# One decoder block on one core: a latent's spread in another PSUM group, two weight splits placed later, and the order of some additions and last sums

## The chip, the cores and the metric

The kernel runs on one core of one Trainium2 chip. The metric is the device time of one execution in microseconds (us). The kernel before took a median of 786.34 us in three runs (785.65 to 786.46).

## The reference, cut to what matters

One block of depth 1 on 512 tokens with a model width of 1024, everything in fp32:

```
n      = rmsnorm(x);  proj = n @ w_in            # gq gk gv gr, gates, cq, ckv, kr, z_ma, z_mb
y_gla  = rmsnorm(gla_forward + gla_backward) * silu(gr)          # 4 heads, dk 128, dv 256, chunked
q      = rmsnorm(cq) @ w_uq;  k, v = rmsnorm(ckv) @ w_ukv        # 8 heads, with rotary parts
y_mla  = softmax(q k^T) v
h      = x + (sigmoid(z_ma) * y_gla + sigmoid(z_mb) * y_mla) @ w_out
h      = h + square(relu(rmsnorm(h) @ w_ff1)) @ w_ff2            # 1024 -> 4096 -> 1024
out    = rmsnorm(h) * g_final
```

## The kernel before, in words

**Arithmetic.** fp32 operands are split into a high part (rounded by ScalarE, L96 or L100) and a low part (the rest, by VectorE, L97 or L101). A product is three matmuls: high by high, high by low, low by high (`mm3`, L91 to L93). So every weight tile passes through three steps: a load on SyncE's queue (`weights`, L222), a high half on ScalarE, a low half on VectorE. Staging buffers for raw weights (`wf`) are three; the halves (`wh`, `wl`) have four buffers each.

**Who orders the work.** The program is traced in the order of the code. A scheduler then orders each engine's instructions by priority and by when buffers come free, and adds the semaphore waits. The code overrides it in places: `issued_after` (L103) makes one instruction of an engine stand behind another, `in_program_order` (L113) holds a whole stretch to the traced order, and `tensor_engine_goes_on` (L126) puts TensorE's first instruction of one stretch behind its last one of another. Each engine and each queue runs its own list in order: an instruction that waits holds everything behind it on that engine.

**PSUM.** There are two groups of four banks, `mm` and `at` (`ps`, L80). Projections use `mm`. Scores, gates, sums of squares and the spread of a norm use `at`. A new tile of a group takes the bank whose last user is done.

**First part, per GLA head h = 0..3** (loop at L782). The head's gates come from `gate_parts`; `gla_qk` makes decayed q and k. Then follow `mla_g2` (a projection of z_mb, named zb, multiplied by R on VectorE, L532, and put through tanh on ScalarE, L534, named tb) and `gla_scores` (L476). `gla_scores` makes bd (four 128-column products), copies it to bds on ScalarE (L483), and then makes for each of four key tiles a score tile sc: three matmuls (L491 to L493), a compare-copy of the diagonal on VectorE (L497), and a split (L96, L97). In heads 0, 1 and 3 TensorE is held to zb first and the scores behind it; head 2 does it the other way round. After the scores come the next head's gates (gatef, gateb, L395), in heads 0 to 2.

**The latents** (`latent`, L584). In head 3 the key/value latent ckv and the query latent cq are projected, and the row norm is found by sums of squares, a power on GpSimd (L265) and a diagonal (cqdg, L273). `spread` (L279) multiplies the diagonal by ones so that every partition holds all norms (tile cqrs, a bank of `at`). VectorE multiplies cq by it (cqc, L602), the result is split (cqhl), and the rotary product ro and the query projections read it. The spread is held behind head 3's scores on TensorE. Also in head 3, VectorE makes the rotary keys (krsin, kswap, kr, L665 to L668).

**Output product, norm and transposes** (`rows_product`, L855). The merged rows times w_out, in two column halves, four row tiles i of 128 tokens. In the second half the last four k blocks are kept back, so that the row tiles complete one after another. On completion VectorE adds the tile to the residual h (L905), ScalarE squares, GpSimd takes the power (L182) and VectorE normalises into ms (L922); then TensorE transposes it (mb, L197). Two row tiles share the banks; `evacuate` writes the transposed activations mT, eight times, high on ScalarE (L100), low on VectorE (L101). TensorE goes straight into the first two MLP weight tiles f00 and f01 on the first half of the tokens, then the transposes of rows 2 and 3, then the second half. Tiles f02, f03 and so on follow with all tokens.

**MLP** (four quarters of the 4096 hidden features). Eight tiles f make the hidden activations (`hidden`, relu at L1000, squares behind it). The second product is done in seven block products on 2 x 2 blocks (`ORDER`, L1032), with weight tiles w that are combined and split by `prep`. Their sums gather in PSUM tiles gx, gz, gw and are added to h after each product (`add_rows`, L905). In the last quarter the split for product 2 is prepared after product 7; product 4 goes on in the same bank (gx) whose content product 7's addition reads.

**End** (`last_rows`, L1066, in program order). Products 4 and 2 are done by rows. For each row tile: addition, square of the left half, last sum and power (`row_rstd`, L178, on VectorE and GpSimd), then `out_store` (L1059): left half times norm and gain on VectorE (L1061), right half times norm on ScalarE (L1062), and two stores (L1063, L1064).

Of the kernel before, what the change touches and what calls it, by code (L numbers as in the profile page):

```python
# [15 lines left out]
ALU = mybir.AluOpType  # L16
AX = mybir.AxisListType

P = 128
S = 512  # L20
# [39 lines left out]
def tile_block(ctx: ExitStack, tc: tile.TileContext, t, out: bass.AP):  # L60
# [19 lines left out]
    def ps(tag, name):  # L80
        serial[0] += 1
        return pp.tile([P, S], F32, tag=tag, bufs=4, name=f"{name}_{serial[0]}")
# [39 lines left out]
            prev[ins.engine] = ins.name  # L122

    PE_ONLY = (mybir.EngineType.PE,)

    def tensor_engine_goes_on(start, mid):  # L126

        ins = nc.cur_bb.bb.instructions
        pe = [[i for i in part if i.engine in PE_ONLY] for part in (ins[start:mid], ins[mid:])]
        issued_after(pe[1][0], pe[0][-1].name)  # L130


    ident = one([P, P], F32, "ident")
# [142 lines left out]
            )  # L276
        return diag

    def spread(diag, name):  # L279
        rs = ps("at", f"{name}rs")  # L280
        for x in range(2):
            nc.tensor.matmul(
                rs, ones_r, diag[:, x].rearrange("p a b -> p (a b)"), start=x == 0, stop=x == 1
            )
        return rs
# [298 lines left out]
    def latent(col, n, gcol, name):  # L584
        cs, sqs = [], []
        for j in range(n):
            acc = proj_T(col + j * P, f"{name}{j}")
            c = u2(f"{name}c{j}")
            nc.scalar.activation(c, acc, AF.Copy, scale=gvec[:, gcol + j : gcol + j + 1])
            s = u2(f"{name}s{j}")  # L590
            nc.scalar.activation(s, acc, AF.Square)
            if sqs:
                nc.vector.tensor_tensor(s, s, sqs[-1], op=ALU.add)
            cs.append(c)
            sqs.append(s)
        yield
        diag = feature_rstd(sqs[-1], n * P, name, True)
        yield
        rs = spread(diag, name)
        res = []  # L600
        for j in range(n):
            nc.vector.tensor_tensor(cs[j], cs[j], rs, op=ALU.mult)  # L602
# [179 lines left out]
    for h in range(GH):  # L782
        last = h == GH - 1
        if h:
            g1 = gla_g1(h, (0,))
            waiting = gla_rstd(*waiting)
            g1 += gla_g1(h, (1,))
            y1 += gla_norm(*waiting)
        if h == GH - 2:
            cos, sin = rotary_tables()  # L790
        near, nxt, far = gla_qk(h, parts)
        if last:
            ckv_steps, cq_steps = latent(C_CKV, 2, V_KV, "ckv"), latent(C_CQ, 3, V_Q, "cq")
# [7 lines left out]
        begun = traced()  # L801
        if h == 2:
            sc = gla_scores(near, nxt, far)
            g2.append(mla_g2(2 * h))
        else:
            g2.append(mla_g2(2 * h))
            gated_at = traced()
            sc = gla_scores(near, nxt, far)
            tensor_engine_goes_on(begun, gated_at)
        if last:  # L810
            scored_at = traced()
            cq = next(cq_steps)
            tensor_engine_goes_on(gated_at, scored_at)
# [41 lines left out]
    def rows_product(lhs, w, nk, name, first_done, done, flip):  # L855
        for c in range(2):
            accs = [ps(("mm", "at")[c], f"{name}{c}{i}") for i in range(NT)]

            def piece(i, k2, wh, wl):
                tok = slice(i * P, (i + 1) * P)  # L860
                for kk in range(2):
                    k = 2 * k2 + kk
                    mm3(accs[i], lhs[k][:, 0, tok], lhs[k][:, 1, tok], wh[:, kk, :], wl[:, kk, :],
                        k == 0, k == nk - 1)

            staggered = 2 if c == 1 else 0
# [24 lines left out]

            whole, first, rest = slice(0, 4), slice(0, 2), slice(2, 4)
            for i in range(2):
                part(i, whole)
# [17 lines left out]
    def first_half_square(i):  # L912
        hparts[i] = sm(f"hp{i}", 4)
        ms_rows[i] = u4(f"ms{i}", F32, (P, D))
        square_half(hrow[i], 0, hparts[i], ms_rows[i])

    def normed(i):
        m = ms_rows[i]
        square_half(hrow[i], 1, hparts[i], m)
        rs = row_rstd(hparts[i])  # L920
        for c in range(2):
            nc.vector.tensor_scalar(  # L922
                m[:, c * S : (c + 1) * S], hrow[i][:, c * S : (c + 1) * S], rs, None, op0=ALU.mult
            )

    def flipped(i):
        fm.rows(i, ms_rows[i])
        if i % 2 == 1:
            fm.evacuate(i // 2)

    begun = rows_product(merged, t["w_out"][0], KD, "wo", first_half_square, normed, flipped)


# [59 lines left out]
    def hidden(qd, j):  # L993

        if qd == 0 and j < 2:
            acc = early[j][2]
        else:
# [54 lines left out]
    def out_square(i, cols, final=True):  # L1052
# [3 lines left out]
            return row_rstd(p)  # L1056
        nc.vector.scalar_tensor_tensor(p[:, 2:3], p[:, 1:2], 1.0 / D, p[:, 2:3], op0=ALU.mult, op1=ALU.add)

    def out_store(i):  # L1059
        o, rs = ms_rows[i], hparts[i][:, 3:4]  # L1060
        nc.vector.scalar_tensor_tensor(o[:, 0:S], hrow[i][:, 0:S], rs, gfin[:, 0:S], op0=ALU.mult, op1=ALU.mult)  # L1061
        nc.scalar.activation(o[:, S:D], o[:, S:D], AF.Copy, scale=rs)  # L1062
        nc.sync.dma_start(out[0, i * P : (i + 1) * P, 0:S], o[:, 0:S])  # L1063
        (nc.scalar if i == 1 else nc.sync).dma_start(out[0, i * P : (i + 1) * P, S:D], o[:, S:D])  # L1064

    def last_rows(left, right4, right2, x_accs):  # L1066
# [6 lines left out]
        e_accs = [ps("mm", f"ge{rb}") for rb in range(2)]  # L1073
        parts = e_accs[1], ps("at", "gend")
        block_product(2, left, right2, e_accs, True, 0)
        out_store(2)
        add_rows(0, 0, e_accs[0])
        out_square(0, slice(0, S))
        out_store(3)
        cols = [slice(x * HT, (x + 1) * HT) for x in range(2)]  # L1080
        for x in range(2):
# [20 lines left out]
    for qd in range(NQ):  # L1102
# [14 lines left out]
        for n, m in enumerate(ORDER):  # L1117
# [50 lines left out]
```

## Time and profile before

| what | value |
|---|---|
| median of three runs | 786.34 us |
| the profiled execution | 786.52 us |
| its span, first to last instruction | 784.8 us |
| TensorE's mean granted clock | 0.997 |
| TensorE busy | 773.0 us |
| VectorE busy | 546.6 us |
| ScalarE busy | 409.9 us |
| GpSimd busy | 103.7 us |

The span is what the trace covers; the time of the execution has 1.7 us more. Engines are named PE (TensorE), PEld (its weight loads), DVE (VectorE), ACT (ScalarE), POOL (GpSimd) and SP (SyncE); a q behind the name is the engine's sequencer, which also issues transfers. A row of a timeline has the start in us from the span's begin, the duration, the engine, the line of the kernel, the operation, out<-in by the program's names, the shape, how many such instructions the row holds, and in brackets the idle time of the engine before it with what ended it. Matmul ends are modelled, so two rows may overlap; the distance from one start to the next is what a matmul costs when nothing waits.

### The profile page before, as it was taken

Reading aid. Unit: us, or ns where it says so; the run is one execution under the profiler, and the core shown is the slowest. Engines: PE = TensorE matmul, PEld = TensorE weight load, DVE = VectorE, ACT = ScalarE, POOL = GpSimd, SP = SyncE. Lnnn points to the kernel's source line nnn. Section 1 sums busy time; section 2 is a strip of 40 time slices with the busy share of each in tenths; the row PEclk is TensorE's granted clock in tenths of the full one; section 3 lists DMA queues with packets and bytes.
Section 4 is the critical chain, followed back from the end, with each engine's and each line's share of the span. In section 5 each row is a group of like instructions: output and inputs, shape, how many; then the busy total and the mean of one; then the engine's idle time right before and its main releaser. Section 6 shows DMA issues by size and latency. Waiting matters only on the chain.

```text
span 784.8 us, 10007 instructions
## 1 busy us (share of the span) xinstructions
PE 773.0 (98%) x3736; PEld 648.1 (83%) x3736; DVE 546.6 (70%) x839; ACT 409.9 (52%) x685; POOL 103.7 (13%) x168
## 2 busy tenths in 40 slices
PE   9999999999999999999999999999999999999996
PEld 7888888888888887888888898888888888888885
DVE  7767656675565459899963668875787578848684
ACT  7464624532652336798852456535554465436644
POOL 1023203203031214211120000000000000000013
PEclk9999999999999999999999999999999999999998
DMA  7633133133213321523133381154106410460002
GB/s 255 169 87 107 34 93 90 54 98 104 81 54 84 71 58 36 135 55 108 28 133 88 106 266 54 54 184 138 50 13 206 139 51 27 168 182 0 28 2 107
DMA packets 102385, 74.47 MB, mean 95 GB/s; under 512 B 14976, under 2 KB 86656, under 8 KB 102336
## 3 DMA queue, kind: packets, MB, share of 16 engines
q1 hardware_dynamic: 101248, 70.66, 30.8%
q10 hardware_dynamic: 864, 2.38, 0.9%
q0 software_dynamic: 224, 0.79, 0.3%
q8 instruction: 29, 0.48, 0.3%
q14 instruction: 20, 0.16, 0.1%
HBM read 69.62 MB, written 2.10 MB: 91 GB/s over the span
## 4 chain that ended last, share of the span: by engine, by line
PE 92%; issue 3%; DVE 3%; ACT 1%; POOL 1%; POOLq 0%; DVEq 0%; ACTq 0%
PE f L92 7%; PE f L93 7%; PE f L91 7%; PE gx L91 4%; PE gx L93 4%; PE gx L92 4%; PE gv L317 3%; PE gr L91 2%; PE gr L93 2%; PE gz L91 2%; PE za L93 2%; PE gr L92 2%; PE gz L93 2%; PE za L91 2%; PE gz L92 2%
## 5 line engine op out<-in xcount | busy, mean ns | idle before, releaser
L952 DVE TENSOR_TENSOR w<-w,w 128x1024 f32<-128x1024 f32 x32 | 38.8, 1221 | 0.3
L1114 POOL DMA_DIRECT2D gfin<-in_g_final x1 | 0.7, 653 | 282.4 <-PE f L93 282.4
L741 ACT ACTIVATE e<-s,top 128x512 f32<-128x512 f32 x32 | 21.9, 684 | 6.0 <-DVE top L738 5.1
L97 DVE TENSOR_TENSOR pT<-tp,pT 128x512 fp32r<-128x512 f32 x32 | 21.7, 679 | 0.5 <-ACT pT L96 0.4
L905 DVE TENSOR_TENSOR h<-gx,h 128x512 f32<-128x512 f32 x32 | 21.6, 684 | 0.4 <-PE gx L93 0.3
L738 DVE TENSOR_REDUCE top<-s 128x1 f32<-128x512 f32 x32 | 21.7, 679 | 0.1
L96 ACT ACTIVATE pT<-tp 128x512 fp32r<-128x512 f32 x32 | 18.9, 592 | 3.1 <-PE tp L755 2.9
L755 PE MATMUL tp<-ident,e 128*128 128x128 f32 x128 | 19.2, 273 | 0.1
L91 PE MATMUL av<-pT,v 128*128 128x256 f32 x64 | 19.3, 301 | 0.0
L755 PEld LDWEIGHTS tp<-ident,e 128*128 128x128 f32 x128 | 15.4, 141 | 3.9 <-DVE pT L97 0.5
L773 POOL TENSOR_TENSOR tb<-tb,g 128x512 f32<-128x512 f32 x8 | 11.1, 1381 | 56.9 <-DVE tb L772 43.8
L1000 ACT ACTIVATE fa<-f 128x512 f32<-128x512 f32 x32 | 18.5, 577 | 0.0
L92 PE MATMUL av<-pT,v 128*128 128x256 f32 x64 | 18.4, 288 | 0.0
L532 DVE TENSOR_TENSOR za<-za,R 128x512 f32<-128x512 f32 x8 | 5.5, 691 | 18.4 <-PE za L93 18.4
L93 PE MATMUL av<-pT,v 128*128 128x256 f32 x64 | 18.1, 283 | 0.0
L96 ACT ACTIVATE gbh<-y 128x512 fp32r<-128x512 f32 x16 | 10.1, 632 | 14.0 <-DVE y L1017 14.0
L448 POOL TENSOR_TENSOR qk<-qkf,e3f 128x256 f32<-128x256 f32 x8 | 7.8, 973 | 63.8 <-DVE qkf L440 63.8
L91 PE MATMUL s<-kbuf,q 128*128 128x512 f32 x32 | 13.7, 429 | 0.3 <-DVE pT L97 0.3
L96 ACT ACTIVATE b_00h<-w 128x1024 fp32r<-128x1024 f32 x7 | 7.4, 1060 | 12.5 <-PE gz L93 6.0
L1009 ACT ACTIVATE px<-fa 128x256 f32<-128x256 f32 x32 | 13.4, 418 | 1.0
L96 ACT ACTIVATE b_10h<-w 128x1024 fp32r<-128x1024 f32 x7 | 7.4, 1060 | 12.1 <-PE gz L93 6.0
L96 ACT ACTIVATE b_20h<-w 128x1024 fp32r<-128x1024 f32 x7 | 7.4, 1060 | 12.1 <-PE gz L93 6.0
(1460 smaller groups left out, 2807.3 us busy)
## 6 DMA issues: line engine op xcount, KB each, us to landing
w<-in_w_ff SPq DMA_DIRECT2D x64, 256.0 KB, 3.6
x<-in_xt SPq DMA_DIRECT2D x8, 256.0 KB, 5.0
vw<-in_w_in SPq DMA_DIRECT2D x8, 256.0 KB, 5.2
q<-ro SPq DMA_DIRECT2D x16, 128.0 KB, 4.9
h<-in_x ACTq DMA_DIRECT2D x4, 512.0 KB, 5.3
out<-ms SPq DMA_DIRECT2D x7, 256.0 KB, 2.3
gr0f<-in_w_in SPq DMA_DIRECT2D x1, 512.0 KB, 5.0
za0f<-in_w_in SPq DMA_DIRECT2D x1, 512.0 KB, 6.1
```

The lines of the kernel that those rows point to most:

```text
L91: nc.tensor.matmul(acc, lh, rh, start=start, stop=False, skip_group_check=onto)
L92: nc.tensor.matmul(acc, lh, rl, start=False, stop=False, skip_group_check=onto)
L93: nc.tensor.matmul(acc, ll, rh, start=False, stop=stop, skip_group_check=onto)
L96: nc.scalar.activation(hi, src, AF.Copy)
L97: rest.tensor_tensor(lo, src, raw(hi), op=ALU.subtract)
L317: nc.tensor.matmul(v_accs[i], a[:, i * P : (i + 1) * P], b, start=k == 0 and x == 0, stop=k == KD - 1 and x == 2)
L738: nc.vector.tensor_reduce(top, acc, axis=AX.X, op=ALU.max, negate=True)
L741: nc.scalar.activation(e, acc, AF.Exp, bias=top, accum_out=tot)
L755: nc.tensor.transpose(tp[:, k * P : (k + 1) * P], e[:, k * P : (k + 1) * P], ident)
L905: nc.vector.tensor_tensor(hc, acc, hc, op=ALU.add)
L952: nc.vector.tensor_tensor(wq[dst][g], wq[x][g], wq[y][g], op=op)
L1000: nc.scalar.activation(a, acc, AF.Relu)
```

## The change

1. `spread` takes the group of its bank as an argument; the latents' spread uses `mm` instead of `at`. In heads 0, 1 and 3 the projection zb is still first on TensorE with the scores behind it, but its multiply and tanh are traced after the scores.
2. Weight tiles f02 and f03: their splits on ScalarE and VectorE are put behind the normalising of row tile 3 and behind the second evacuation.
3. In `rows_product` row tile 3 does one kept k block ahead of the transposes of row tile 1 and three behind it, instead of two and two.
4. Last quarter: VectorE's part of preparing product 2's weights is put behind both additions of product 7.
5. The left half of the output is a function of its own (`out_left`), and that of row 0 is placed between row 1's two sums.

```diff
+    SPLITTERS = (mybir.EngineType.Activation, mybir.EngineType.DVE)
-    def tensor_engine_goes_on(start, mid):
+    def goes_behind(late, early, engines):
         ins = nc.cur_bb.bb.instructions
-        pe = [[i for i in part if i.engine in PE_ONLY] for part in (ins[start:mid], ins[mid:])]
-        issued_after(pe[1][0], pe[0][-1].name)
+        for e in engines:
+            a, b = [[i for i in ins[x:y] if i.engine == e] for x, y in (early, late)]
+            if a and b:
+                issued_after(b[0], a[-1].name)
...
-    def spread(diag, name):
-        rs = ps("at", f"{name}rs")
+    def spread(diag, name, tag="at"):
+        rs = ps(tag, f"{name}rs")
...
-        rs = spread(diag, name)
+        rs = spread(diag, name, "mm")
...
-            g2.append(mla_g2(2 * h))
-            gated_at = traced()
+            began = traced()
+            zb = proj_T(C_ZB + 2 * h * P, f"zb{2 * h}")
+            projected = traced()
             sc = gla_scores(near, nxt, far)
-            tensor_engine_goes_on(begun, gated_at)
+            scored = traced()
+            goes_behind((projected, scored), (began, projected), PE_ONLY)
+            g2.append(gated(zb, f"b{2 * h}")[1])
...
-            whole, first, rest = slice(0, 4), slice(0, 2), slice(2, 4)
...
-                part(2 + i, first)
+                part(2 + i, slice(0, 2 - i))
                 flip(i)
-                part(2 + i, rest)
+                part(2 + i, slice(2 - i, 4))
...
+        elif qd == 0 and j in (2, 3):
+            at = traced()
+            begun = proj_begin(w1, j * P, f"f{qd}{j}")
+            goes_behind((at, traced()), span["norm", NT - 1] if j == 2 else span["evacuate", 1], SPLITTERS)
+            acc = proj_run(begun, mT)
...
+    def out_left(i):
+        o, rs = ms_rows[i], hparts[i][:, 3:4]
+        nc.vector.scalar_tensor_tensor(o[:, 0:S], hrow[i][:, 0:S], rs, gfin[:, 0:S], op0=ALU.mult, op1=ALU.mult)
...
         for x in range(2):
             out_square(1, cols[x], x == 1)
-        for x in range(2):
-            out_store(x)
+            if x == 0:
+                out_left(0)
+        out_store(0)
+        out_left(1)
+        out_store(1)
...
+            adding = traced()
             for rb in range(2):
                 block_product(m, left, right[m], accs, begin, rb)
...
             if behind:
+                added = traced()
                 right[ahead] = prep(ahead, qd)
+                goes_behind((added, traced()), (adding, added), SPLITTERS[1:])
```

`span["norm", i]` and `span["evacuate", half]` are the traced stretches of `normed(i)` and `fm.evacuate(half)`.

More of the change, by code (lines that the diff above doesn't have):

```diff
@@ L800, in tile_block @@
             v = gla_v(1)
-        begun = traced()
         if h == 2:
@@ L805, in tile_block @@
         else:
-            g2.append(mla_g2(2 * h))
-            gated_at = traced()
+            began = traced()
+            zb = proj_T(C_ZB + 2 * h * P, f"zb{2 * h}")
+            projected = traced()
             sc = gla_scores(near, nxt, far)
-            tensor_engine_goes_on(begun, gated_at)
+            scored = traced()
+            goes_behind((projected, scored), (began, projected), PE_ONLY)
+            g2.append(gated(zb, f"b{2 * h}")[1])
         if last:
-            scored_at = traced()
+            spreading = traced()
             cq = next(cq_steps)
-            tensor_engine_goes_on(gated_at, scored_at)
+            goes_behind((spreading, traced()), (projected, scored), PE_ONLY)
             kbuf = rotary_k()
@@ L890, in complete @@
                 done(i)
-            whole, first, rest = slice(0, 4), slice(0, 2), slice(2, 4)
             for i in range(2):
-                part(i, whole)
+                part(i, slice(0, 4))
                 complete(i)
             for i in range(2):
-                part(2 + i, first)
+                part(2 + i, slice(0, 2 - i))
                 flip(i)
-                part(2 + i, rest)
+                part(2 + i, slice(2 - i, 4))
                 complete(2 + i)
@@ L915, in first_half_square @@
         square_half(hrow[i], 0, hparts[i], ms_rows[i])
+    span = {}
     def normed(i):
+        at = traced()
         m = ms_rows[i]
@@ L924, in normed @@
             )
+        span["norm", i] = at, traced()
     def flipped(i):
@@ L928, in flipped @@
         if i % 2 == 1:
+            at = traced()
             fm.evacuate(i // 2)
+            span["evacuate", i // 2] = at, traced()
     begun = rows_product(merged, t["w_out"][0], KD, "wo", first_half_square, normed, flipped)
@@ L996, in hidden @@
             acc = early[j][2]
+        elif qd == 0 and j in (2, 3):
+            at = traced()
+            begun = proj_begin(w1, j * P, f"f{qd}{j}")
+            goes_behind((at, traced()), span["norm", NT - 1] if j == 2 else span["evacuate", 1], SPLITTERS)
+            acc = proj_run(begun, mT)
         else:
@@ L1075, in last_rows @@
         block_product(2, left, right2, e_accs, True, 0)
+        out_left(2)
         out_store(2)
@@ L1078, in last_rows @@
         out_square(0, slice(0, S))
+        out_left(3)
         out_store(3)
```

1 line of the change is left out of this document (removed).

## The prediction, as it went on record

> **What bounds the kernel now.** I read the page's busy shares first, then TensorE's list of waits, then the timelines around each of them.
>
> ```profile
> span 784.8 us, 10007 instructions
> PE 773.0 (98%) x3736; PEld 648.1 (83%) x3736; DVE 546.6 (70%) x839; ACT 409.9 (52%) x685; POOL 103.7 (13%) x168
> ```
>
> TensorE is busy for 773.0 of 784.8 us. An edit that leaves its matmuls as they are can win only where TensorE stands still, or behind its last matmul. The list of TensorE's waits says where it stands:
>
> ```profile
> PE cqrs L282 <- DVE sc L97: 1.2, 1, 1.2
> PE f L92 <- DVE mT L101: 1.1, 1, 1.1
> PE s L91 <- DVE pT L97: 0.3, 1, 0.3
> PE sc L491 <- ACT bds L483: 0.2, 1, 0.2
> PE gx L91 <- DVE h L905: 0.2, 1, 0.2
> ```
>
> Columns: total, times, longest. Four of these five (not the third) are places that the diff touches; together they show 2.7 us. The profiled run took 786.52 us, 1.7 outside its span, and lies 0.18 above the median of the runs shown (786.34). My sum is made against 786.52. About 0.2% (1.6 us) is what a measurement of this kernel can tell from no change.
>
> **Part 1: the latent's spread and head 3's scores.** Timelines of VectorE, ScalarE and TensorE, start and duration in us:
>
> ```profile
> 293.49 0.69 DVE L666 TENSOR_TENSOR kswap<-kswap,krsin 64x512 f32<-64x512 f32 x1
> ...
> 295.67 1.89 DVE L97 TENSOR_TENSOR sc<-sc,sc 128x512 fp32r<-128x512 f32 x3
> 297.47 0.29 DVE L497 COPY_PREDICATED sc<-after,bds 128x128 f32<-128x128 int32 x1
> 297.67 1.28 DVE L602 TENSOR_TENSOR cqc<-cqc,cqrs 128x512 f32<-128x512 f32 x2
> ```
> ```profile
> 292.97 0.63 ACT L534 ACTIVATE tb<-zb 128x512 f32<-128x512 f32 x1 [2.26 <-DVE zb L532]
> 293.51 0.58 ACT L483 ACTIVATE bds<-bd 128x512 f32<-128x512 f32 x1
> ...
> 298.38 1.24 ACT L96 ACTIVATE cqhl<-cqc 128x512 fp32r<-128x512 f32 x2
> ```
> ```profile
> 299.49 0.39 PE L91 MATMUL ro<-cqhl,wr0h 128*128 128x512 f32 x1
> ```
> ```profile
> 476.41 0.39 PE L91 MATMUL f<-mT,f05h 128*128 128x512 f32 x1
> 476.63 0.39 PE L92 MATMUL f<-mT,f05h 128*128 128x512 f32 x1
> ```
>
> Today cqrs takes a bank of the scores' group and waits until VectorE has split a score (1.2 us). In the changed program as built it waits for its own diagonal alone, which VectorE has made before it comes to kswap at 293.49. The second wait, sc behind bds, goes too: bds stood in ScalarE's queue behind tb, which waited 2.26 us for zb; the gating is now traced after the scores and bds runs in that idle time.
>
> What is late next is ro, the first consumer of the spread latent. Its operand cqhl comes from ScalarE, cqc from VectorE, and cqc stands behind the scores' work there. That queue starts at 293.49 with, as built, a compare-copy, kswap, and then three times compare-copy and split. From start to start a split takes (297.47 − 295.67) / 3 = 0.60 us and a compare-copy 297.67 − 297.47 = 0.20, so cqc starts at 293.49 + 4 × 0.60 + 4 × 0.20 = 296.7 and ends, half of 1.28 later, at 297.3. ScalarE's half of 1.24 makes it 298.0, TensorE's start 298.1. Before it was 299.49, with one matmul more ahead of it (a gla3o matmul, moved behind ro, costs its 476.63 − 476.41 = 0.22 later). Gain 299.49 − 0.22 − 298.1 = 1.2; I take off 0.1 for the slower restart after a wait: **−1.05**. TensorE still waits here, so the bounds are −1.4 (both listed waits gone, nothing new) and −0.3 (VectorE's queue 0.8 longer than worked out).
>
> **Part 2: the same edit in heads 0 and 1** has no wait to remove there. It puts zb's multiply between the first and the second compare-copy on VectorE, and tb between the first two score splits on ScalarE:
>
> ```profile
> 75.98 1.29 DVE L97 TENSOR_TENSOR sc<-sc,sc 128x512 fp32r<-128x512 f32 x2
> ```
> ```profile
> 77.42 0.47 PE L395 MATMUL gateb<-z,gate_b 128*128 128x512 f32 x1
> ```
>
> The second split ends at 75.98 + 1.29 = 77.27, and gateb, which takes that score's bank, starts at 77.42. Delayed by tb (0.54 from start to start, by the rows of tb and bds above), gateb becomes possible at 77.96. As built, TensorE has one zb matmul to put ahead of it, 0.22 us. So 0.54 − 0.22 = 0.3 us are lost, in each of two heads: **+0.6**, between 0 (cover found) and +0.8. The gates themselves come 0.54 later; only the next head's q and k need them, after four more projections.
>
> **Part 3: two weight splits of the MLP.** f02's split goes behind the normalising of row tile 3, f03's behind the second evacuation, and the transposes of row tile 1 go one k block (three matmuls, 0.7 us) forward.
>
> ```profile
> 443.25 1.06 ACT L96 ACTIVATE f02h<-f02f 128x1024 fp32r<-128x1024 f32 x1
> ```
> ```profile
> 444.94 1.22 DVE L97 TENSOR_TENSOR f02l<-f02f,f02h 128x1024 fp32r<-128x1024 f32 x1
> 446.07 3.22 DVE L101 SCALAR_TENSOR_TENSOR mT<-mb,gvec,mT 128x256 fp32r<-128x256 f32 x8
> ...
> 451.76 0.89 DVE L922 TENSOR_SCALAR ms<-h,hp 128x512 f32<-128x512 f32 x2 [0.66 <-POOL hp L182]
> 453.61 3.23 DVE L101 SCALAR_TENSOR_TENSOR mT<-mb,gvec,mT 128x256 fp32r<-128x256 f32 x8 [0.97 <-ACT mT L100]
> ```
> ```profile
> 446.61 0.39 PE L92 MATMUL f<-mT,f00h 128*128 128x256 f32 x1 [1.08 <-DVE mT L101]
> ...
> 454.43 0.28 PE L92 MATMUL f<-mT,f00h 128*128 128x256 f32 x1
> ```
>
> VectorE's first mT moves from 446.07 to 444.94, where f02l stood: 1.13 earlier, against a wait of 1.08. ScalarE's half takes f02h's place at 443.25 and is in time. **−1.1**.
>
> Both splits must then fit in later. f02l (1.22) now stands between row 3's norm and the second evacuation. That norm ends at 451.76 + 0.89 = 452.65, or 451.5 when all of it comes 1.1 earlier; f02l ends at 452.7. The first of eight mT (3.23 / 8 = 0.4) ends at 453.1; TensorE wants it at 454.43 − 1.1 = 453.3. It fits with 0.2 to spare, and a little more since f03l no longer stands inside row 3's norm. Without that cover up to 1.1 comes back: bounds −1.2 and 0.
>
> The move also changes SyncE's queue: f05's load needs f02's buffer, so the sixteen w loads pass it. That is the rival on the slow side, below.
>
> **Part 4: additions ahead of the last w split.**
>
> ```profile
> 766.54 1.82 DVE L97 TENSOR_TENSOR b_30l<-w,b_30h 128x1024 fp32r<-128x1024 f32 x1 [1.74 <-ACT b_30h L96]
> 768.28 0.68 DVE L905 TENSOR_TENSOR h<-gx,h 128x512 f32<-128x512 f32 x1
> 768.88 1.21 DVE L97 TENSOR_TENSOR b_31l<-w,b_31h 128x1024 fp32r<-128x1024 f32 x1
> ```
> ```profile
> 768.42 0.39 PE L93 MATMUL gx<-b_31h,gd 128*128 128x512 f32 x1
> 769.02 0.50 PE L91 MATMUL gx<-b_30h,gd 128*128 128x512 f32 x1 [0.21 <-DVE h L905]
> ...
> 771.87 0.39 PE L91 MATMUL ge<-b_30h,ga 128*128 128x512 f32 x1
> ```
>
> The add goes before b_30l and is done by 767.2. TensorE's next matmul starts at 768.42 + 0.22 = 768.64 instead of 769.02: 0.38, and 0.1 of restart: **−0.45**, bounds −0.5 and −0.2. Both splits end some 0.7 later, b_31l at 770.8, ahead of ge at 771.4: hidden.
>
> **Part 5: last sums.** Row 0's left product (L1061) now stands ahead of row 1's last sum instead of behind it.
>
> ```profile
> L182 POOL TENSOR_TENSOR hp<-hp,mhalf x8: 548/562/1034, 437.3 to 779.0; 128x1 f32<-128x1 f32 x8
> ```
> ```profile
> 778.81 0.74 DVE L1061 SCALAR_TENSOR_TENSOR ms<-h,hp,gfin 128x512 f32<-128x512 f32 x1
> 780.00 0.75 DVE L1061 SCALAR_TENSOR_TENSOR ms<-h,hp,gfin 128x512 f32<-128x512 f32 x1 [0.44 <-POOL hp L182]
> ```
> ```profile
> 778.98 0.99 POOL L182 TENSOR_TENSOR hp<-hp,mhalf 128x1 f32<-128x1 f32 x1 [1.48 <-DVE hp L179]
> 780.75 0.38 ACTq L1064 DMA_DIRECT2D out<-ms  x1
> ```
> ```profile
> DMA to landing us min/median/max: 2.0/2.3/2.9
> ```
>
> GpSimd's power takes 0.56 us as the median and 0.99 here, where L1061 runs beside it. With L1061 done first it should take 0.56: −0.43, less some 0.05 that the sum may queue behind L1061. The last store is the slowest of the eight (2.9 against 2.3), issued together with its twin just behind row 0's two. Row 0's left store now leaves 0.7 earlier (L1061's length), so about half of that 0.6 should go: −0.3. **−0.7**, bounds −0.9 and 0 (the power slow for another reason).
>
> [...]
>
> **Sum**: −1.05 + 0.6 − 1.1 − 0.45 − 0.7 = −2.7, so 786.52 − 2.7 = 783.8 us. All bounds at once: 782.5 to 786.8.
>
> **Rivals.** (a) *The wait at ro takes the place of the two removed*: VectorE's queue decides ro, not the bank; part 1 gives only 0.3: 784.6. For it: cqc is already at the end of that queue. Against: the kr product leaves the queue ahead of cqc, and bds no longer holds the first compare-copy. Chance 0.13. (b) *The second evacuation waits for f02l*: the spare 0.2 is not there, part 3 gives about 0: 784.9. Chance 0.10. (c) *Parts 1 and 3 both fail* and little but the end is left: 785.7. Chance 0.07. (d) *Slower: f05 comes late.*
>
> ```profile
> 446.64 12.00 SPq L948 DMA_DIRECT2D w<-in_w_ff x16
> ```
>
> The sixteen loads end their issue at 458.6. Should they not start earlier, f05's load goes out then and not before them, and ScalarE's f05h, in front of gbh and the next relus, holds its queue until it lands. TensorE wants f05 at 476.41, and its two halves need 1.06 + 1.22 (f02's rows), so the landing decides from 474 on, 15 us after issue. Each microsecond beyond costs one: landing at 477 takes the whole gain, landing at 479 gives 788.8. Against: in the built program the first four w loads wait for nothing of this stage, so the queue is through sooner. Chance 0.03. (e) That the spread's new bank is not free is excluded by the waits of the built program.
>
> **How the numbers follow.** Forecast 783.8 with chance 0.67, its own spread about ±0.9 from the bounds; the rivals hold 0.33. The range 782.6 to 785.1 takes in (a), (b) and most of the forecast, and leaves out (c), (d) and the far ends. Faster by over 0.2% means under 784.8: the forecast nearly whole (0.65), most of (a) (0.10), half of (b) (0.05) and a little of (c) (0.02): 0.82. Within 0.2%: 0.14. Slower: 0.04.
>
> **What would show it.** In TensorE's waits: cqrs, gx and sc gone, f under 0.2, a new one of ro on ScalarE's cqhl near 0.9, gateb near 0.3 twice. On GpSimd the last power at 0.56. In the second evacuation no wait of f. Wrong would be a wait of f above 0.5, ro near 299, or a power still at 1.0.

## The result and the profile after

The changed kernel takes 783.47 us (median of 6 runs, 783.31 to 784.54) against 786.40 for the kernel before (6 runs beside them, 785.65 to 787.37): a ratio of 0.9965, 95% interval 0.9952 to 0.9978. The forecast was 783.8 with a range from 782.6 to 785.1. The profiled execution took 783.52 us, 3.0 less than that of before.

The page of the changed kernel, span and busy times, and then its whole list of TensorE's waits (total, times, longest):

```profile
span 781.8 us, 10005 instructions
PE 772.8 (99%) x3736; PEld 648.5 (83%) x3736; DVE 544.2 (70%) x839; ACT 410.1 (52%) x685; POOL 104.1 (13%) x168
```
```profile
PE warm L310 <- POOL ident masks.py:199: 1.5, 1, 1.5
PE ro L91 <- ACT cqhl L96: 0.3, 1, 0.3
PE s L91 <- DVE pT L97: 0.3, 1, 0.3
```

TensorE's busy time is unchanged (773.0 and 772.8); the span is 3.0 shorter. The waits of cqrs, f, sc and gx are gone, and a new one of ro has come. That tells which waits went, not what each was worth. For this one needs instructions that are the same in both kernels and stand at the borders of the stages. TensorE's timeline of the kernel before (start, duration):

```profile
289.99 0.39 PE L93 MATMUL zb<-xT,zb6l 128*128 128x512 f32 x1
...
318.25 0.39 PE L93 MATMUL gla3o<-sc,gv 128*128 128x512 f32 x1
...
449.42 0.32 PE L92 MATMUL f<-mT,f00h 128*128 128x256 f32 x1
...
765.93 0.39 PE L91 MATMUL gx<-b_30h,gd 128*128 128x512 f32 x1
...
777.34 0.28 PE L93 MATMUL gend<-b_31h,ga 128*128 128x256 f32 x1
```

and of the changed kernel:

```profile
290.76 0.40 PE L93 MATMUL zb<-xT,zb6l 128*128 128x512 f32 x1
...
298.42 0.50 PE L91 MATMUL ro<-cqhl,wr0h 128*128 128x512 f32 x1 [0.32 <-ACT cqhl L96]
...
317.57 0.39 PE L93 MATMUL gla3o<-sc,gv 128*128 128x512 f32 x1
...
447.62 0.32 PE L92 MATMUL f<-mT,f00h 128*128 128x256 f32 x1
...
764.06 0.39 PE L91 MATMUL gx<-b_30h,gd 128*128 128x512 f32 x1
...
774.98 0.28 PE L93 MATMUL gend<-b_31h,ga 128*128 128x256 f32 x1
```

The first row of each is the last matmul ahead of head 3's scores, the second gla3o row the last one of that stage. Read at these rows and at a few more starts from both timelines:

| border (TensorE's start) | before | after | lead of after | stage's part | forecast |
|---|---|---|---|---|---|
| first gv of gv03h, end of the start-up | 22.73 | 22.90 | +0.17 | +0.17 | none |
| zb6l, ahead of head 3's scores | 289.99 | 290.76 | +0.77 | +0.60 | +0.6 (part 2) |
| last gla3o | 318.25 | 317.57 | −0.68 | −1.45 | −1.05 (part 1) |
| f00h, last of the first half | 449.42 | 447.62 | −1.80 | −1.12 | −1.1 (part 3) |
| first gx of b_30h and gd | 765.93 | 764.06 | −1.87 | −0.07 | 0 |
| last matmul | 777.34 | 774.98 | −2.36 | −0.49 | −0.45 (part 4) |
| ScalarE's last store issued | 780.75 | 777.94 | −2.81 | −0.45 | −0.4 (part 5) |
| end of the span | 784.8 | 781.8 | −3.0 | −0.2 | −0.3 (part 5) |

Behind the last matmul, the changed kernel's VectorE, GpSimd and ScalarE:

```profile
775.71 0.75 DVE L1076 SCALAR_TENSOR_TENSOR ms<-h,hp,gfin 128x512 f32<-128x512 f32 x1
```
```profile
776.61 0.55 POOL L185 TENSOR_TENSOR hp<-hp,mhalf 128x1 f32<-128x1 f32 x1 [1.48 <-DVE hp L182]
```
```profile
777.94 0.38 ACTq L1082 DMA_DIRECT2D out<-ms  x1
```

Row 0's left product (L1076) is over at 776.46, before the power begins, and the power takes 0.55 where it took 0.99. Four of the five terms of the sum are within 0.15 us of the forecast. The one that is not is head 3: −1.45, outside the bounds given for it (−1.4 to −0.3). The experiments take the parts one at a time.

One execution used below, the profiled one of tail_alone, ran at a granted clock of 0.655; its time is left out, and its trace is read for durations off TensorE alone.

### The profile page after: what moved, and what is told of

Read it like the earlier page. It is cut to its first block, busy times and chain, and to the rows that moved or that the text cites. A ratio compares the mean times of both kernels' runs of the same rounds, so it can differ in the third digit from the quotient of the medians.

```text
span 781.8 us, 10005 instructions
## 1 busy us (share of the span) xinstructions
PE 772.8 (99%) x3736; PEld 648.5 (83%) x3736; DVE 544.2 (70%) x839; ACT 410.1 (52%) x685; POOL 104.1 (13%) x168
## 4 chain that ended last, share of the span: by engine, by line
PE 94%; issue 3%; DVE 2%; ACT 1%; POOL 0%; POOLq 0%
PE f L92 8%; PE f L93 7%; PE f L91 7%; PE gx L91 4%; PE gx L93 4%; PE gx L92 4%; PE gv L320 3%; PE gr L91 2%; PE gr L93 2%; PE wo L93 2%; PE wo L91 2%; PE gr L92 2%; PE gz L93 2%; PE za L92 2%; PE gz L91 2%
```

## The experiments

Each kernel is the kernel before or the changed one with a single edit; only the two attempts at the end have more. Single parts are worth about 1 us, little more than the width of the intervals, so sizes are read from the borders above and the times only say whether they agree.

### The bank alone

```
-    def spread(diag, name):
-        rs = ps("at", f"{name}rs")
+    def spread(diag, name, tag="at"):
+        rs = ps(tag, f"{name}rs")
...
-        rs = spread(diag, name)          # in latent
+        rs = spread(diag, name, "mm")
```

> The kernel before with one edit: the latents' spread takes its bank from the other group; the gating stays ahead of the scores. Theory (VectorE's queue sets ro, the bank only says where TensorE stands still): the wait of cqrs goes, but ro still starts at 299.4 to 299.6, since the latent's first multiply on VectorE stays behind three compare-copies, the kr product and three score splits. As built, three gla3o matmuls that stood behind ro now stand ahead of it, 0.23 us each, so ro's wait is about 0.9 and TensorE is 0.7 us ahead from 315 us on. The wait of sc on bds (0.2) stays. Time 0.7 us below before. Rival (the bank is what counts): ro at 298.3 and a gain of 1.2 to 1.4, the whole of the changed kernel's gain in this stage.

Measured: 785.90 us, ratio 0.9995 (0.9986 to 1.0004). TensorE's timeline:

```profile
296.61 0.50 PE L91 MATMUL gla3o<-sc,gv 128*128 128x512 f32 x1 [0.67 <-DVE sc L97]
...
299.69 0.39 PE L91 MATMUL ro<-cqhl,wr0h 128*128 128x512 f32 x1
```

The wait of cqrs is gone and 0.67 of it has moved to the first gla3o; ro starts no earlier (299.69, and this execution had come into the stage 0.20 late). The gain of the stage is the three gla3o matmuls that now stand ahead of ro: 0.68. As the theory had it, the bank sets where TensorE stands still and not when ro can begin.

### Head 3's order alone

```
-            g2.append(mla_g2(2 * h))
-            gated_at = traced()
-            sc = gla_scores(near, nxt, far)
+            zb = proj_T(C_ZB + 2 * h * P, f"zb{2 * h}")
+            th = None if last else gated(zb, f"b{2 * h}")[1]
+            gated_at = traced()
+            sc = gla_scores(near, nxt, far)
...
+            g2.append(gated(zb, f"b{2 * h}")[1] if last else th)
```

> The kernel before with one edit: in head 3 alone zb's multiply and tanh are traced behind the scores; the spread keeps its old bank group and heads 0 and 1 are as before. Theory (VectorE's queue sets ro): bds runs on ScalarE at about 291.4, the first compare-copy at about 292.7 instead of 294.2, so the first score split ends near 294.7 and cqrs, which still takes a bank of the scores' group, waits at most 0.3 us; ro starts at 297.7 to 298.0 and TensorE is 1.2 to 1.4 us ahead from 315 us on. Time 1.3 below before. Rival (the bank counts): cqrs still waits about 1 us and the gain is 0.2 to 0.4, that of sc's wait alone.

Measured: 785.39 us, ratio 0.9992 (0.9983 to 1.0001). TensorE's timeline:

```profile
295.06 0.71 PE L282 MATMUL cqrs<-cqdg,ones_r 128*128 128x512 f32 x2
...
298.03 0.39 PE L91 MATMUL ro<-cqhl,wr0h 128*128 128x512 f32 x1
```

cqrs, in its old bank group, waits no more, and ro starts at 298.03: the stage from zb6l to the last gla3o takes 26.88 us against 28.26 before and 26.81 with the bank as well. As these profiles stand, the order does all but 0.07 of part 1. But the times show 0.6, less than half of the 1.4 of the profile (the interval reaches to 1.3). The next comparison shows that the 1.4 compares two unlike executions.

### A collision that comes and goes

Six profiles hold the unchanged order of head 3's gating: that of before and those of bank_alone, flip_alone, late_alone, adds_alone and one_input. Their stages differ more than the edits explain. VectorE's second cqdg product and GpSimd's second half of the wq0 split, in the kernel before:

```profile
290.84 1.50 DVE L273 TENSOR_TENSOR cqdg<-ident,cqrl 128x512 fp32r<-128x512 f32 x1
```
```profile
290.79 1.00 POOL L97 TENSOR_TENSOR wq0l<-wq0f,wq0h 128x384 fp32r<-128x384 f32 x1 [1.08 <-ACT wq0h L96]
```

and in late_alone, whose code is the same in this stage:

```profile
291.19 0.68 DVE L283 TENSOR_TENSOR cqdg<-ident,cqrl 128x512 fp32r<-128x512 f32 x1
```
```profile
291.19 1.55 POOL L97 TENSOR_TENSOR wq0l<-wq0f,wq0h 128x384 fp32r<-128x384 f32 x1 [1.11 <-ACT wq0h L96]
```

In these rows one of the two runs at its own speed (1.00 or 0.68) and the other is held up (1.55 or 1.50). GpSimd went ahead where its recorded start leads by 0.04 or 0.05 us, and VectorE where that lead is 0.02 or less, in every profile in which nothing was moved to force it. What the two contend for, no run shows. Below, an execution has met the collision when GpSimd went ahead and VectorE's product was held up. The chip doesn't decide it: flip_alone met the collision and adds_alone, measured on the same one, did not. VectorE's queue to ro starts 0.8 earlier or later by that. The stage from zb6l to the last gla3o, by order and by who went ahead:

| kernel | who went ahead | stage, us |
|---|---|---|
| before, flip_alone | GpSimd | 28.26, 28.25 |
| late_alone, adds_alone, one_input | VectorE | 27.61, 27.56, 27.59 |
| bank_alone | GpSimd | 27.59 |
| order3_alone | VectorE | 26.88 |
| changed, keep01 | VectorE | 26.81, 26.81 |

The profile of before met the collision and that of the changed kernel did not. Like against like, part 1 is worth 27.59 − 26.81 = 0.78, and 28.26 − 27.59 = 0.67 of its 1.45 are the luck of two executions.

The two halves have to be read the same way. order3_alone did not meet the collision, so the order is worth 27.59 − 26.88 = 0.71 there, of 0.78. bank_alone met it, and against before, which met it too, the bank is worth 28.26 − 27.59 = 0.67, of the 0.71 that the whole change brings with the collision (after_hit, next). So each half alone gives nearly the whole gain in the execution in which it was seen, though only the order brings ro forward: with the bank alone TensorE does three gla3o matmuls while ro is not ready. The bank alone without the collision and the order alone with it were not seen.

Two kernels test the collision.

The first puts the collision into the changed kernel:

```
         for x, c in ((0, raw(rh)), (1, rl)):
+            if name == "cq" and x == 1:
+                nc.vector.tensor_copy(rl, c)
             nc.vector.tensor_tensor(
```

> The changed kernel with one small VectorE copy (128 by 4) put between the two cqdg products, so that GpSimd's wq0l starts ahead of the second one in every execution. [...] Rival (the changed order has slack for it, as the gating no longer stands ahead of bds): ro within 0.3 of 298.42, time 783.5.

Measured: 784.63 us, ratio to the kernel before 0.9980 (0.9970 to 0.9989), 1.2 above the changed kernel (by the ratios, as they were measured at different times). Its VectorE and GpSimd:

```profile
291.19 1.37 DVE L278 TENSOR_TENSOR cqdg<-ident,cqrl 128x512 fp32r<-128x512 f32 x1
```
```profile
290.99 1.03 POOL L97 TENSOR_TENSOR wq0l<-wq0f,wq0h 128x384 fp32r<-128x384 f32 x1 [1.11 <-ACT wq0h L96]
```

The stage takes 27.55, 0.74 more than in the changed kernel. The copy itself holds little of it: from the first cqdg to the product behind the second it is 2.10 (290.39 to 292.49), and 2.03 in before, which met the collision without a copy. The changed order has no slack for the collision. Why the medians lie 1.2 apart and the stage only 0.74 stays open. Against before, which met it too, the gain is 28.26 − 27.55 = 0.71.

The second takes the collision out of the kernel before:

```
+            raising = traced()
             for _ in up_units(0):
                 pass
+            goes_behind((raising, traced()), (scored_at, latent_at), SPLITTERS[:1])
```

> The kernel before with one edit outside the change: ScalarE's split of wq0, and so GpSimd's second half of it, is held behind the latent's splits, so that GpSimd no longer runs beside VectorE's product cqdg. Theory (in three of six profiles in which this stage has the code of before, GpSimd's wq0l starts 0.04 or 0.05 us ahead of the second cqdg and that product takes 1.50 instead of 0.68): cqdg takes 0.68, the wait of cqrs is 1.0, and counted from 280 us on, TensorE is 0.6 us ahead of the profile of before at 297 us. Time 0.3 below before, half of the 0.6, since the unchanged code meets the collision in about half of its executions. Rival 1 (cqdg is slow for another reason): 1.50 stays. Rival 2 (wq0l, moved to about 303 us, collides with the kbuf products and ro is late there): a new wait after 303 us and no gain.

Measured: 786.88 us, ratio 1.0013 (1.0004 to 1.0022): slower. The second cqdg takes 0.68 and the stage 27.58, as the theory said, but the gain is lost 3 us on. Its list of waits has a new row, and VectorE:

```profile
PE gla3ss L265 <- DVE gla3sq L581: 0.4, 1, 0.4
```
```profile
319.83 0.90 DVE L581 TENSOR_TENSOR gla3sq<-gla3sq,gla3sq 128x512 f32<-128x512 f32 x1
```

Set beside adds_alone, which has this stage as in the kernel before and did not meet the collision, and counted from zb6l, gla3sq starts 0.44 later (29.72 us on, 29.28 there) and takes 0.22 longer (0.90 for 0.68) beside a GpSimd split (wk2l, 317.91 to 320.19). By the rows the late start comes through ScalarE: behind the moved split its own work is 0.4 to 0.9 later (tb 0.87), and its split of ro 0.7, which VectorE's then follows. TensorE waits at gla3ss for both. The second rival named the collision as the cause and another place; what it makes up is at most a third of the loss. Why the median lies 0.8 above that of before and not level, as in the profile (784.9 against 784.8), stays open.

### Heads 0 and 1 put back

```
             zb = proj_T(C_ZB + 2 * h * P, f"zb{2 * h}")
+            th = None if last else gated(zb, f"b{2 * h}")[1]
             projected = traced()
...
-            g2.append(gated(zb, f"b{2 * h}")[1])
+            g2.append(gated(zb, f"b{2 * h}")[1] if last else th)
```

> The changed kernel with one edit undone: in heads 0 and 1 zb's multiply and tanh stand ahead of the scores again; head 3 is as changed. Theory: gateb goes back to 0.2 us of extra time in both heads instead of 0.2 for zb and 0.3 for gateb, so each head is 0.29 us shorter and the total is 0.58 below the changed kernel: 782.9 us, span 781.2. Rival (the gates' tanh, 0.5 us earlier or later, shifts something in the next projections and the gain is given back): 783.4, with a new wait between 78 and 130 us.

Measured: 783.43 us (5 runs, 782.94 to 784.09), ratio 0.9966 (0.9953 to 0.9978). The page and TensorE's timeline:

```profile
span 781.2 us, 10005 instructions
```
```profile
290.17 0.40 PE L93 MATMUL zb<-xT,zb6l 128*128 128x512 f32 x1
```

It comes to head 3's scores at 290.17 instead of 290.76, and the rest runs as in the changed kernel; of the 0.59, 0.05 is the start-up. The two losses of part 2 are real in the profile. The medians (783.43 and 783.47) don't show it; with five and six runs that scatter over 1.2 us they can't tell 0.5.

### The two halves of part 3

```
# late_alone: the two splits held back, transposes where they were
+        elif qd == 0 and j in (2, 3):
+            at = traced()
+            begun = proj_begin(w1, j * P, f"f{qd}{j}")
+            goes_behind((at, traced()), span["norm", NT - 1] if j == 2 else span["evacuate", 1], SPLITTERS)
+            acc = proj_run(begun, mT)
```

> The kernel before with one edit: the splits of f02 and f03 are held behind row tile 3's norm and behind the second evacuation; row tile 1's transposes stay where they were. Theory (VectorE's own queue sets the first evacuation): TensorE's wait of f at 446.6 falls from 1.1 to under 0.2 and TensorE is 1.1 to 1.2 us ahead from 450 us on, with no wait in the second evacuation. Time 1.15 below before; the earlier transposes add nothing. Rival (the transposes also have to come forward): ScalarE's first half is late, a wait of f of 0.4 to 0.8 stays, and the gain is 0.4 to 0.7.

Measured: 785.05 us, ratio 0.9986 (0.9976 to 0.9995). The wait of f is gone, and from the last gla3o to the last f00h of the first half TensorE takes 448.00 − 317.99 = 130.01 against 131.17 before: 1.16 gained. Nothing comes back in the second evacuation. Holding the splits back does the whole of part 3.

```
# flip_alone: transposes one k block forward, nothing held back
-                part(2 + i, first)
+                part(2 + i, slice(0, 2 - i))
                 flip(i)
-                part(2 + i, rest)
+                part(2 + i, slice(2 - i, 4))
```

> The kernel before with one edit: row tile 1's transposes come one k block forward; nothing is held back by hand. As built, the planner itself then puts f02's split behind the first evacuation, so f02l stands ahead of row tile 3's sum and f03l between that sum and its norm on VectorE. Theory: the wait at the first evacuation (1.1) goes, but row tile 3's norm ends about 0.9 later than in the changed kernel, which has 0.2 to spare, so 0.6 to 0.8 us come back as a wait in the second evacuation, and the gain is 0.3 to 0.6. Rival (the second evacuation has more to spare than worked out): no such wait and a gain of 1.1.

Measured: 786.49 us, ratio 1.0003 (0.9994 to 1.0013): no gain that the times can tell. Its wait and VectorE:

```profile
PE mb L197 <- DVE ms L921: 0.7, 1, 0.7
```
```profile
450.63 1.21 DVE L97 TENSOR_TENSOR f03l<-f03f,f03h 128x1024 fp32r<-128x1024 f32 x1
452.28 0.88 DVE L921 TENSOR_SCALAR ms<-h,hp 128x512 f32<-128x512 f32 x2 [0.44 <-POOL hp L182]
```

The first wait goes here too (1.14 gained by 449 us), because the planner itself moves both splits, but f03l lands ahead of row tile 3's norm, the transposes wait 0.7 for that norm, and 0.84 of the 1.14 is given back; 0.30 is left in the profile, the low end of what was expected. This is close to rival (b): there the second evacuation waits for f02l, here its transposes wait for row tile 3's norm, which a split holds up in the same way. Freeing the place ahead of the first evacuation is not enough: the splits must also be held off that norm.

### Parts 4 and 5 alone

```
# adds_alone
+            adding = traced()
             for rb in range(2):
...
+                added = traced()
                 right[ahead] = prep(ahead, qd)
+                goes_behind((added, traced()), (adding, added), SPLITTERS[1:])
```

> The kernel before with one edit: the additions stand ahead of the splits of the w product behind them. Theory: the wait of gx on h at 769.02 goes and TensorE's last matmul starts 0.45 to 0.5 earlier (776.85 to 776.9); nothing else moves. Rival (the splits, 0.7 later, become the wait): ge's first matmul at 771.87 waits for b_31l and the gain is under 0.2.

Measured: 785.80 us, ratio 0.9993 (0.9983 to 1.0002). The wait of gx is gone and TensorE has gained 0.50 between the first gx of b_30h and the last matmuls; no later wait appears.

```
# tail_alone: row 0's left product ahead of row 1's last sum
         for x in range(2):
             out_square(1, cols[x], x == 1)
-        for x in range(2):
-            out_store(x)
+            if x == 0:
+                out_left(0)
+        out_store(0)
+        out_left(1)
+        out_store(1)
```

> The kernel before with one edit: row 0's left product stands ahead of row 1's last sum. Theory: GpSimd's last power takes 0.55 instead of 0.99, the last stores leave 0.44 earlier after TensorE's last matmul (2.97 instead of 3.41), and the last landing takes 2.8 instead of 2.9: 0.5 to 0.6 us less from the last matmul to the last landing (5.75 instead of 6.33). Rival 1 (the last landing follows row 0's earlier store fully): 2.6, and 0.75 less in all. Rival 2 (the power is slow for another reason): 0.99 stays and nothing is gained but the landing's 0.1.

Measured: 785.57 us (the nine other executions), ratio 0.9992 (0.9982 to 1.0002). GpSimd's last power:

```profile
1103.88 0.55 POOL L182 TENSOR_TENSOR hp<-hp,mhalf 128x1 f32<-128x1 f32 x1 [2.49 <-DVE hp L179]
```

The theory's 0.55, with this part of the change alone. The longest of its eight stores takes 2.8 to land, as the theory had it, and not the 2.6 of rival 1.

one_input keeps the old sequence and leaves out the final gain in row 0's left half:

```
+        if i == 0:
+            nc.vector.tensor_scalar(o[:, 0:S], hrow[i][:, 0:S], rs, None, op0=ALU.mult)
+        else:
+            nc.vector.scalar_tensor_tensor(o[:, 0:S], hrow[i][:, 0:S], rs, gfin[:, 0:S], op0=ALU.mult, op1=ALU.mult)
```

> The kernel before, in its old sequence, but row 0's left product leaves out the multiplication by the final gain: one SBUF input instead of two, a tensor-by-scalar product. It still runs beside GpSimd's last power. Theory (two SBUF inputs on VectorE hold GpSimd off): the power takes 0.55 although VectorE is busy beside it. Rival 1 (a one-input product from SBUF to SBUF holds it off too, for its own shorter time of about 0.45): the power takes 0.65 to 0.85. Rival 2 (the power is slow for a reason other than the neighbour): 0.99.

Measured, VectorE and GpSimd:

```profile
778.42 0.48 DVE L1062 TENSOR_SCALAR ms<-h,hp 128x512 f32<-128x512 f32 x1
```
```profile
778.58 0.72 POOL L182 TENSOR_TENSOR hp<-hp,mhalf 128x1 f32<-128x1 f32 x1 [1.48 <-DVE hp L179]
```

Rival 1: this one-input product holds the power off too (0.72, against 0.55 in tail_alone), for its own shorter time (0.48, against 0.74 in before). The power ends 778.58 + 0.72 − 778.42 − 0.48 = 0.40 behind the product's end; with two inputs (before) it ended 0.42 behind. Leaving out the second input does not free the power; why it is held off, neither run shows.

### Two attempts at a faster version

In the changed kernel ro still waits 0.3, and VectorE's second compare-copy stands behind kswap. The next kernel is keep01 with krsin, kswap and kr held behind the score splits:

```
+            turning = traced()
             kbuf = rotary_k()
+            goes_behind((turning, traced()), (projected, scored), SPLITTERS[1:])
```

> The changed kernel with heads 0 and 1 as before, and head 3's rotary products of k (krsin, kswap, kr) held behind the score splits on VectorE. Theory (VectorE's queue sets ro): the second compare-copy no longer waits for kswap (0.7), the latent's first multiply starts about 0.6 earlier, ro starts at 297.0 to 297.3 against 297.82 in the version without this edit; two gla3o matmuls (0.23 each) move behind ro, so TensorE is 0.1 to 0.3 us ahead of that version from 315 us on: 782.7 to 782.9 us. Rival (the moved products make kbuf late): a new wait of the first scores s on kbuf after 312 us, and the gain of this edit is lost or negative.

Measured: 785.06 us, ratio 0.9986 (0.9978 to 0.9995): 1.6 slower than keep01. ro starts at 296.95, earlier than expected, and it doesn't help. The waits and VectorE's kbuf products:

```profile
PE uk L91 <- ACT ro L96: 0.7, 1, 0.7
PE uv L91 <- DVE zb L535: 0.6, 1, 0.6
```
```profile
303.95 4.01 DVE L101 SCALAR_TENSOR_TENSOR kbuf<-kr,gvec,kbuf 64x512 fp32r<-64x512 f32 x4
```

In keep01 the four kbuf products take 2.76 from 301.68 on. Here they come 2.3 later and take 4.01, and what stands behind them on VectorE (roa, zb's multiply) is late for TensorE at uk and uv. The wait was moved from ro to its readers and grew.

The last kernel has the late wq0 split of wq_late as well:

```
+            raising = traced()
             for _ in up_units(0):
                 pass
+            goes_behind((raising, traced()), (spreading, turning), SPLITTERS[:1])
```

> The version before with ScalarE's and GpSimd's split of wq0 held behind the latent's splits as well. Theory: in a profile whose execution has no collision at cqdg this changes nothing (within 0.1 us of the version without it); it takes away the executions that have one, so its median lies 0 to 0.4 below that version's and its runs scatter less: 782.6 us. Rival (wq0l collides with the kbuf products instead): up to 1 us later roa, a wait of ro's readers, 783.3.

Measured: 784.77 us, ratio 0.9984 (0.9975 to 0.9993). The second cqdg takes 0.69 without GpSimd beside it, but the wait of uk is 1.2 and the last matmul is 0.4 behind that of the version without the late split. Neither attempt beats the changed kernel; keep01 equals it in the times.

## Why the prediction was right, and where not

**The whole.** 783.8 forecast, 783.47 measured, by the forecast case: parts 1, 3, 4 and 5 win, part 2 loses. How near the numbers lie is in part luck. Like against like the five terms are 0.60 − 0.78 − 1.12 − 0.49 − 0.64 = −2.43 against −2.7 forecast, an estimate of 784.1; the two profiled executions differ by 3.0 because that of before met a collision (0.67) and the other did not. The medians, 2.9 apart with an interval of 1.7 to 3.8, can't tell the two.

**Part 1** (−1.05 forecast, −1.45 measured): the mechanism was right, the size was not, and two errors stand against each other. "VectorE's queue decides ro" holds: the bank alone leaves ro where it was, the order alone brings it to 298.03. The first step that failed is the point of departure, "That queue starts at 293.49 with, as built, a compare-copy, kswap": I took the start from the profile of before as if it were fixed. The row a little ahead of it, a cqdg of 1.50 where its twin takes 0.69, showed that the queue had just been held up beside GpSimd. Without that, the first compare-copy of the changed kernel comes 0.8 earlier in its stage. VectorE's queue in the changed kernel:

```profile
291.58 0.68 DVE L276 TENSOR_TENSOR cqdg<-ident,cqrl 128x512 fp32r<-128x512 f32 x1
...
293.44 0.30 DVE L500 COPY_PREDICATED sc<-after,bds 128x128 f32<-128x128 int32 x1
293.77 0.69 DVE L669 TENSOR_TENSOR kswap<-kswap,krsin 64x512 f32<-64x512 f32 x1
294.49 0.30 DVE L500 COPY_PREDICATED sc<-after,bds 128x128 f32<-128x128 int32 x1
...
297.03 0.67 DVE L605 TENSOR_TENSOR cqc<-cqc,cqrs 128x512 f32<-128x512 f32 x1
```

The first compare-copy runs at 293.44 although everything upstream is 0.77 later, so at 292.67 in the clock of before.

The second step that failed is the length of the queue, "293.49 + 4 × 0.60 + 4 × 0.20", or 3.2: it takes 297.03 − 293.44 = 3.59. From start to start kswap costs 0.72 and the two compare-copies around it 0.33 each, where the sum has 0.60 and 0.20, taken from the splits and the last compare-copy; kswap's 0.72 (293.49 to the next start at 294.21) stood in the profile of before. after_hit, where the collision is forced, shows this error by itself:

```profile
293.71 0.30 DVE L502 COPY_PREDICATED sc<-after,bds 128x128 f32<-128x128 int32 x1
...
297.31 0.68 DVE L607 TENSOR_TENSOR cqc<-cqc,cqrs 128x512 f32<-128x512 f32 x1
```

It comes into the stage 0.20 later than before, so its queue starts at 293.51 in the clock of before, where the prediction had it; the queue takes 3.60, and the gain is 0.71 instead of 1.05. In the changed kernel the early start hides this: ro starts at 298.42 − 0.77 = 297.65 in the clock of before, 0.45 ahead of the 298.1 worked out, and its new wait is 0.3 in the list and not 0.9 (0.6 with its slow restart: from the gla3o matmul ahead of ro to ro's second matmul TensorE takes 298.76 − 297.71 = 1.05, where two steps of 0.23 take 0.46). Like against like, part 1 is worth 0.71 to 0.78, less than forecast. Rival (a), ro's wait in place of the two removed ones, had a gain of 0.3 and is refuted.

**Part 2** (+0.6 forecast, +0.60 measured): shown by keep01, which takes 0.54 of it back. The loss in head 0 is where it was worked out:

```profile
78.10 0.47 PE L398 MATMUL gateb<-z,gate_b 128*128 128x512 f32 x1
```

gateb started at 77.42 before; with the 0.17 of the start-up taken off it is 0.51 later (0.54 worked out), and one zb matmul has gone ahead of it. The sign named for this, a wait of gateb near 0.3 twice, is not in the list of waits.

**Part 3** (−1.1 forecast, −1.12 measured): right, f02l ends ahead of the second evacuation as worked out. late_alone shows that the held splits do it, not the earlier transposes. Rival (d) never came near: f05's load was issued at 451.76, its split began at 462.3, and TensorE used it at 474.6.

**Part 4** (−0.45 forecast, −0.49 measured): right, alone and in the whole.

**Part 5** (−0.7 forecast, about −0.6 measured): the power fell by 0.44 as forecast; the last landing gained 0.1 to 0.2 (0.1 by the list of landings, 0.2 by the end of the span) instead of 0.3. The longest of the eight takes 2.8 (2.9 before) though row 0's left store leaves earlier: whether the two last stores, issued within 0.03 us of each other, hold each other up was not tried.

**The start-up** (+0.17) was in no term and is not the change: over twelve profiles of kernels with the same start, the first gv of gv03h begins between 22.34 and 23.49.

## What to carry to other kernels

Before a wait is priced from one profile, look for instructions in its chain that take much longer than their twins: here a 1.50 beside a 0.69 of the same shape was a collision, and the executions that met it differ from those that did not by some 0.02 us in one start. Price each operation of a queue by its own row, not by a neighbour's. Measure parts between two instructions that are the same in both kernels, and compare executions that met the same collisions. An operation moved out of the way takes its neighbours on other engines along: three of the moves tried here (wq_late, keep01_kr, flip_alone) removed the delay they aimed at and made another.

## What the runs showed of the hardware

TensorE's start differs between executions. The first four gv matmuls, which follow each other without a wait, in the kernel before, flip_alone and after_hit:

```profile
4.96 1.67 PE L317 MATMUL gv<-gv00h,xT 128*128 128x512 f32 x4
```
```profile
4.96 2.05 PE L317 MATMUL gv<-gv00h,xT 128*128 128x512 f32 x4
```
```profile
4.97 1.19 PE L322 MATMUL gv<-gv00h,xT 128*128 128x512 f32 x4
```

The second four start at 6.47, 6.81 and 6.00, the ninth at 7.39, 8.15 and 7.02. So the second four take 0.92 in before, 0.23 each, and 1.34 in flip_alone, where the first of them starts 0.43 behind the matmul ahead of it (6.81 and 6.38). The pace thus changes at a different place in each execution. By the ninth matmul flip_alone is 1.13 behind after_hit, and the end of the start-up lies 1.15 apart (23.49 and 22.34). What sets the pace, no row shows: the granted clock of before is 1.00 from 0 to 6 us as from 6 to 12 us.

In the ten profiles that were not forced, GpSimd went first at a recorded lead of 0.04 or 0.05 us (three profiles) and VectorE at 0.02 or less (seven), and with it went 0.67 us of this kernel. How often executions without a profile meet that collision was not measured: three of six profiles in the old order did, and none of the four in the changed order (changed, order3_alone, keep01, keep01_kr) in which it was not forced.
